# Moving the rotary tables, a diagonal and one accumulator bank in a hybrid attention block

## The chip, the cores and the metric

The kernel runs on one core of a Trainium2 chip. The metric is the device time of one execution in microseconds (us), as the median of several runs; less is better. A core has five engines that run side by side and wait for each other by semaphores: TensorE (PE in the profile, its weight loads PEld) multiplies matrices into eight accumulator banks of 128 x 512 fp32; VectorE (DVE) and ScalarE (ACT) work on tiles of 128 partitions and read the banks; GpSimd (POOL) works on tiles and issues some transfers; SyncE (SP) issues the other transfers.

## What is computed

One block of a model with 512 tokens and 1024 features, all in fp32. Cut to what matters here:

```python
n = rmsnorm(h, g_mix)
gq, gk, gv, gr, z_gf, z_gb, cq, ckv, kr, z_ma, z_mb = split(n @ w_in)
y_gla = gla_branch(gq, gk, gv, gr, z_gf, z_gb, ...)   # 4 heads, gated linear attention, both directions
q = rmsnorm(cq, g_q) @ w_uq                           # 8 heads; 64 plain and 32 rotary features each
kv = rmsnorm(ckv, g_kv) @ w_ukv                       # keys (64) and values (128) of each head
k_rope = rope(kr, positions)                          # one rotary key for all heads
y_mla = softmax(q @ k.T * 96**-0.5) @ v
merged = sigmoid(z_ma) * y_gla + sigmoid(z_mb) * y_mla
h = h + merged @ w_out
h = h + square(relu(rmsnorm(h, g_mlp) @ w_ff1)) @ w_ff2
return rmsnorm(h, g_final)
```

`rope(x)` turns pairs of features by an angle: it needs the cosine and sine of position times frequency.

## The kernel before, in words

Every matrix product is made of three products (`mm3`, lines 87 to 90): each operand is split into a high part, rounded for TensorE's fast format, and the low rest; high x high, high x low and low x high are summed into one bank. A split takes ScalarE for the high part and VectorE (in places GpSimd) for the low one (`split`, lines 92 to 94; `split_scaled`, 96 to 98).

The work goes in this order: the first input projections; the three large ones (gr, za, gv) by a seven-product scheme for 2 x 2 blocks; the four heads of the linear attention (GLA), with the projections of the latents cq and ckv and of the gates in between; the softmax attention (MLA) of eight heads in pairs; the output product with w_out; the two feed-forward products in four quarters.

The change lies where GLA ends and MLA begins, in the straight stretch for the last GLA head, `h = GH - 1` (lines 1305 to 1340). There stand, in the order of the text:

- `ckv_.sums()` (line 803) sums the squares of the key latent into a bank (`ckvss`), and VectorE and GpSimd make 1/rms of it; `ckv_.diagonals()` (line 811) lets VectorE turn these 512 numbers into two diagonal matrices (`ckvdg`, line 292), in five instructions; `ckv_.spread()` (line 818) multiplies them with ones on TensorE, so that the scale of each token stands in every partition (`ckvrs`, line 301); `ckv_.normed()` scales the latent by it and splits it.
- `gla_state(h, keys)` (line 574): 12 matmuls into one bank, and a copy of the bank by ScalarE (`gla3s`, line 584), which `gla_out` reads on TensorE (line 742).
- `rotary.tables()` (line 858): two ScalarE activations, `sin` (860) and `cos` (861), from angles that were made long before. Their function is not in the table that ScalarE holds, so a table load goes ahead; the next tanh (line 380) loads the old table again.
- `over_rms` (line 375) scales the late gates 4 and 5 on VectorE; `rotary_k()` (line 891) turns the rotary key on VectorE, in four instructions that read `sin` and `cos` (lines 894 to 897); `rotary_k_split()` splits it into `kbuf`.
- `rotary_begin`, `rotary_q`, `up_T`, `up_units` (line 1023): loads, splits and products of the rotary query (`ro`), and for each pair of heads of the plain query (`uq`), the key (`uk`) and the value (`uv`); these are units of a generator, so that later pairs can be put between attention steps.
- the gates z_mb of 128 features each: `zb6` and `zb7` are loaded and split by `begin` and run by `proj_run`; `zb7` is the last, run right ahead of the first scores.

What sets the order: up to this stretch's end TensorE, VectorE and ScalarE keep the order of the text (`in_program_order`, lines 1341 to 1343); GpSimd too. In the attention that follows, a scheduler orders the steps, helped by `goes_behind` pairs; from the output product on the order of the text holds again. SyncE's queue is ordered by the scheduler except for a few pairs.

The eight banks are two pools of four by tag, "mm" and "at". Banks are handed out from the free ones when the scheduler comes to the first use; the use waits until the last reader of the bank's earlier tile is done. In the attention the scores (`s`) and the transposed probabilities (`tp`) take "at" banks, the up-projections, the value products (`av`) and GLA's turns (`y`) take "mm" banks. `begin` always takes "mm"; `proj_begin` takes a tag.

Of the kernel before, what the change touches and what calls it, by code (L numbers as in the profile page):

```python
# [18 lines left out]
P = 128  # L19
# [16 lines left out]
C_ZA, C_ZB = 3776, 4800  # L36
# [20 lines left out]
def tile_block(ctx: ExitStack, tc: tile.TileContext, t, out: bass.AP):  # L57
# [10 lines left out]
    def u2(name, dt=F32, shape=(P, S)):  # L68
        return tl(list(shape), dt, "u2", 29, name)
# [7 lines left out]
    def ps(tag, name):  # L77
        serial[0] += 1
        return pp.tile([P, S], F32, tag=tag, bufs=4, name=f"{name}_{serial[0]}")
# [7 lines left out]
    def mm3(acc, lh, ll, rh, rl, start, stop, onto=False):  # L87
        nc.tensor.matmul(acc, lh, rh, start=start, stop=False, skip_group_check=onto)  # L88
        nc.tensor.matmul(acc, lh, rl, start=False, stop=False, skip_group_check=onto)  # L89
        nc.tensor.matmul(acc, ll, rh, start=False, stop=stop, skip_group_check=onto)  # L90
# [16 lines left out]
    def traced():  # L107
        return len(nc.cur_bb.bb.instructions)
# [111 lines left out]
    def weights(src, name):  # L220
        k, w = src.shape
        nk = k // P
        wf = stage(nk, w, name)
        nc.sync.dma_start(wf, src.rearrange("(k p) w -> p k w", p=P))
        wh, wl = halves(nk, w, name)
        split(wh, wl, wf)
        return wh, wl

    w_in = t["w_in"][0]

    def proj_begin(w, col, name, tag="mm"):
        wh, wl = weights(w[:, col : col + P], name)
        return wh, wl, ps(tag, name)

    def begin_late(col, name, tag="mm", w=None):

        wf = stage(KD, P, name)
        nc.sync.dma_start(wf, (w_in if w is None else w)[:, col : col + P].rearrange("(k p) w -> p k w", p=P))
        wh, wl = halves(KD, P, name)
        nc.scalar.activation(wh, wf, AF.Copy)  # L240

        def lows():
            nc.vector.tensor_tensor(wl, wf, raw(wh), op=ALU.subtract)

        return (wh, wl, ps(tag, name)), lows

    def proj_run(begun, src, half=None, ks=range(KD)):
        wh, wl, acc = begun
        c = slice(0, S) if half is None else slice(half * 256, half * 256 + 256)
        for k in ks:  # L250
            mm3(acc[:, c], wh[:, k, :], wl[:, k, :], src[k][:, 0, c], src[k][:, 1, c], k == 0, k == KD - 1)
        return acc
# [120 lines left out]
    def over_rms(acc, name):  # L373
        z = u2(f"z{name}")
        nc.vector.tensor_tensor(z, acc, R, op=ALU.mult)
        return z

    def half_tanh(z, name):
        th = u2(f"t{name}")
        nc.scalar.activation(th, z, AF.Tanh, scale=0.5)  # L380
        return th
# [192 lines left out]
    def gla_state(h, keys):  # L574

        half, at = h // 2, (h % 2) * GDV
        c = slice(at, at + GDV)
        acc = ps("at", f"gla{h}st")
        for j in range(NT):
            tok = slice(j * P, (j + 1) * P)  # L580
            mm3(acc[:, (j // 2) * GDV : (j // 2 + 1) * GDV], keys[:, 0, tok], keys[:, 1, tok],
                v[j, half][:, 0, c], v[j, half][:, 1, c], j % 2 == 0, j % 2 == 1)
        state = u2(f"gla{h}s")
        nc.scalar.activation(state, acc, AF.Copy)
        return state
# [194 lines left out]
    class Latent:  # L780
# [4 lines left out]
        def begin(self, j):  # L785
            self.begun[j] = proj_begin(w_in, self.col + j * P, f"{self.name}{j}")
# [77 lines left out]
    def rotary_begin():  # L864
        res = []
        for x in range(2):
            wf = stage(3, P, f"wr{x}")
            lo = NOPE + x * HALF
            for k in range(3):
                nc.sync.dma_start(  # L870
                    wf[:, k, :].rearrange("p (h e) -> p h e", h=MH), w_uq[:, k, :, lo : lo + HALF]
                )
            wh, wl = halves(3, P, f"wr{x}")
            split(wh, wl, wf)
            res.append((wh, wl))
        return res
# [14 lines left out]
    def rotary_k():  # L891
        r = slice(64, 96)
        sgn = u2("krsin")
        nc.vector.tensor_scalar(sgn[r], sin[r], cst[r, K_SIGN : K_SIGN + 1], None, op0=ALU.mult)
        nc.vector.tensor_tensor(kswap[r], kswap[r], sgn[r], op=ALU.mult)
        nc.vector.tensor_tensor(kr[r], kr[r], cos[r], op=ALU.mult)
        nc.vector.tensor_tensor(kr[r], kr[r], kswap[r], op=ALU.add)
# [285 lines left out]
    ckv_, cq_ = Latent(C_CKV, 2, V_KV, "ckv"), Latent(C_CQ, 3, V_Q, "cq")  # L1183
# [7 lines left out]
    for n, (a, m) in enumerate(steps[:-4]):  # L1191
# [4 lines left out]
        if steps[n + 1] in fillers:  # L1196
            at = traced()
# [57 lines left out]
    rotary = Rotary()  # L1255
    pooled = traced()
    for h in range(GH - 1):
# [6 lines left out]
        if h < 2:  # L1264
            w_b, lows = begin_late(C_GQ + (h + 2) * P, f"gq{h + 2}")
# [30 lines left out]
        else:  # L1296
# [5 lines left out]
            w_b = begin(C_ZB + 5 * P, "zb5")  # L1302
# [4 lines left out]
    ckv_.sums()  # L1307
    zb5 = proj_run(w_b, xT)
    cq = cq_.normed()
    state = gla_state(h, keys)  # L1310
    cos, sin = rotary.tables()
    late = [over_rms(acc, f"b{f}") for f, acc in ((4, zb), (5, zb5))]
    rotary_k()
    ckv_.diagonals()
    wr = rotary_begin()
    zb = begin(C_ZB + 6 * P, "zb6")
    kbuf = rotary_k_split()
# [9 lines left out]
    ro = rotary_q(accs)  # L1327
    zb = over_rms(proj_run(zb, xT), "b6")
    next(units)
    w_b = begin(C_ZB + 7 * P, "zb7")  # L1330
    g2.append(half_tanh(zb, "b6"))
    first_units = traced()
    for n, _ in enumerate(units):
# [3 lines left out]
    at = traced()  # L1337
# [20 lines left out]
    at = traced()  # L1358
# [4 lines left out]
    for n in range(4 * MH + LAG_C - 1):  # L1363
# [12 lines left out]
        if 2 <= n % 8 < 7:  # L1376
            at = traced()
# [5 lines left out]
        if n in (6, 14):  # L1383
            units = up_units(n // 8 + 2)
            at = traced()
# [4 lines left out]
        if n == 30:  # L1390
            xs_ = wo_accs[1] = [ps("mm", f"wox{rb}") for rb in range(2)]
            at = traced()
# [32 lines left out]
        if n == 17:  # L1425
            at = traced()
# [235 lines left out]
    at = traced()  # L1662
# [9 lines left out]
    at = traced()  # L1672
# [7 lines left out]
    at = traced()  # L1680
# [12 lines left out]
    at = traced()  # L1693
# [8 lines left out]
    for qd in range(NQ):  # L1702
# [14 lines left out]
        for n, m in enumerate(ORDER):  # L1717
# [4 lines left out]
            if m == 2:  # L1722
                accs, begin = [ps("mm", f"gw{qd}{rb}") for rb in range(2)], True
# [3 lines left out]
            else:  # L1727
                accs, begin = (zs_, m == 5) if m in (5, 3) else (xs_, m == 1)
# [20 lines left out]
def build(arrays):  # L1749
    nc = bacc.Bacc("TRN2", target_bir_lowering=False, num_devices=1, dynamic_dma_scratch_size=8192)  # L1750
    t = {
        n: nc.dram_tensor(f"in_{n}", list(a.shape), mybir.dt.from_np(a.dtype), kind="ExternalInput").ap()
        for n, a in arrays.items()
    }
    out = nc.dram_tensor("out_0", [1, S, D], F32, kind="ExternalOutput").ap()
    with tile.TileContext(nc) as tc:
        tile_block(tc, t, out)
    return nc
# [16 lines left out]
```

## Time and profile before

| what | value |
|---|---|
| median of 3 runs | 755.55 us (755.13 to 756.49) |
| the profiled execution | 754.4 us, span of its instructions 752.7 us |
| TensorE clock granted | 0.997 of full |
| first scores of the attention begin | 295.62 us into the span |
| HBM read, written | 83.25 MB, 2.10 MB |

How to read the rows further down: the page's first part gives busy time and share of the span by engine. A row of the waits names who waited, for whom, the sum, how often, the longest. A row of the timeline has start and duration in us, engine, line, operation, `out<-in`, the form (partitions x elements), how often in a row, and in brackets how long the engine had been idle before it and what ended that. Matmuls are pipelined: the next one starts before the end that is shown for the last. A row of the stages (windows) has, for each engine, busy us and the number of instructions.

### The profile page before, as it was taken

Reading aid. Unit: us, or ns where it says so; the run is one execution under the profiler, and the core shown is the slowest. Engines: PE = TensorE matmul, PEld = TensorE weight load, DVE = VectorE, ACT = ScalarE, POOL = GpSimd, SP = SyncE. Lnnn points to the kernel's source line nnn. Section 1 sums busy time; section 2 is a strip of 40 time slices with the busy share of each in tenths; the row PEclk is TensorE's granted clock in tenths of the full one; section 3 lists DMA queues with packets and bytes.
Section 4 is the critical chain, followed back from the end, with each engine's and each line's share of the span. In section 5 each row is a group of like instructions: output and inputs, shape, how many; then the busy total and the mean of one; then the engine's idle time right before and its main releaser. Section 6 shows DMA issues by size and latency. Waiting matters only on the chain.

```text
span 752.7 us, 10206 instructions
## 1 busy us (share of the span) xinstructions
PE 742.9 (99%) x3688; PEld 628.0 (83%) x3688; DVE 580.5 (77%) x842; ACT 457.7 (61%) x776; POOL 165.7 (22%) x238
## 2 busy tenths in 40 slices
PE   9999999999999999999999999999999999999996
PEld 7888888888889888899988988888888888888885
DVE  7777886989787577888897688856696578748795
ACT  7557574686567476978865766345644465345644
POOL 0722110262573522246750100000000000000014
PEclk9999999999999999999999999999999999999998
DMA  9859582611322234458798321461126310650003
GB/s 310 263 124 241 168 175 82 113 29 32 80 57 39 39 85 108 110 146 220 222 194 256 115 66 44 154 182 56 57 80 199 115 56 15 198 152 0 29 0 112
DMA packets 94722, 88.90 MB, mean 118 GB/s; under 512 B 15792, under 2 KB 66992, under 8 KB 94672
## 3 DMA queue, kind: packets, MB, share of 16 engines
q1 hardware_dynamic: 88176, 75.64, 33.8%
q0 software_dynamic: 6208, 12.32, 9.3%
q8 instruction: 29, 0.48, 0.3%
q10 hardware_dynamic: 288, 0.28, 0.1%
q14 instruction: 21, 0.17, 0.1%
HBM read 83.25 MB, written 2.10 MB: 113 GB/s over the span
## 4 chain that ended last, share of the span: by engine, by line
PE 95%; DVE 2%; ACT 1%; issue 1%; POOL 0%; POOLq 0%; ACTq 0%
PE f L88 8%; PE f L89 8%; PE f L90 8%; PE gx L88 4%; PE gx L90 4%; PE gx L89 4%; PE first L330 3%; PE tp L1122 2%; PE gz L88 2%; PE gz L90 2%; PE gz L89 2%; PE zb L88 1%; PE zb L89 1%; PE zb L90 1%; PE av L88 1%; PE s L88 1%
## 5 line engine op out<-in xcount | busy, mean ns | idle before, releaser
L1714 POOL DMA_DIRECT2D gfin<-in_g_final x1 | 0.6, 628 | 283.9 <-PE f L90 283.9
L977 DVE TENSOR_TENSOR w<-w,w 128x1024 f32<-128x1024 f32 x32 | 38.7, 1220 | 0.3
L1102 DVE TENSOR_REDUCE top<-s 128x1 f32<-128x512 f32 x32 | 21.9, 684 | 3.6 <-PE s L90 3.0
L1107 ACT ACTIVATE e<-s,top 128x512 f32<-128x512 f32 x32 | 22.0, 688 | 3.5 <-DVE top L1102 3.4
L1452 DVE TENSOR_TENSOR h<-h,gx 128x512 f32<-128x512 f32 x32 | 21.5, 680 | 1.9 <-PE gx L90 1.8
L94 DVE TENSOR_TENSOR pT<-tp,pT 128x512 fp32r<-128x512 f32 x32 | 21.6, 681 | 1.5 <-ACT pT L93 1.5
L93 ACT ACTIVATE pT<-tp 128x512 fp32r<-128x512 f32 x32 | 18.9, 595 | 2.7 <-PE tp L1122 2.5
L1122 PE MATMUL tp<-ident,e 128*128 128x128 f32 x128 | 19.4, 274 | 0.0
L88 PE MATMUL av<-pT,v 128*128 128x256 f32 x64 | 19.1, 298 | 0.0
L93 ACT ACTIVATE ghb<-y 128x512 fp32r<-128x512 f32 x16 | 10.1, 632 | 14.0 <-DVE y L923 14.0
L1518 ACT ACTIVATE fa<-f 128x512 f32<-128x512 f32 x32 | 18.5, 577 | 0.0
L89 PE MATMUL av<-pT,v 128*128 128x256 f32 x64 | 18.2, 285 | 0.0
L90 PE MATMUL av<-pT,v 128*128 128x256 f32 x64 | 18.1, 283 | 0.0
L1122 PEld LDWEIGHTS tp<-ident,e 128*128 128x128 f32 x128 | 15.2, 140 | 3.3 <-ACT e L1113 0.4
L93 ACT ACTIVATE b_00h<-w 128x1024 fp32r<-128x1024 f32 x7 | 7.4, 1060 | 12.6 <-PE gz L90 6.0
L562 ACT ACTIVATE bds<-bd 128x512 f32<-128x512 f32 x4 | 2.4, 597 | 20.5 <-PE bd L545 20.5
L93 ACT ACTIVATE b_10h<-w 128x1024 fp32r<-128x1024 f32 x7 | 7.4, 1060 | 12.1 <-PE gz L90 6.0
L93 ACT ACTIVATE b_20h<-w 128x1024 fp32r<-128x1024 f32 x7 | 7.4, 1059 | 12.1 <-PE gz L90 6.0
L88 PE MATMUL s<-kbuf,q 96*128 96x512 f32 x32 | 14.1, 441 | 0.0
L1527 ACT ACTIVATE px<-fa 128x256 f32<-128x256 f32 x32 | 13.4, 418 | 1.0
L973 POOL DMA_DIRECT2D w<-in_w_out x10 | 12.3, 1406 | 7.6 <-DVE bo60l L94 6.5
L646 POOL DMA_DIRECT2D gvw<-in_w_in x4 | 4.8, 1226 | 38.7 <-DVE gvw L651 34.0
(1769 smaller groups left out, 2917.6 us busy)
## 6 DMA issues: line engine op xcount, KB each, us to landing
w<-in_w_ff SPq DMA_DIRECT2D x64, 256.0 KB, 3.5
w<-in_w_out POOLq DMA_DIRECT2D x10, 512.0 KB, 9.2
grw<-in_w_in SPq DMA_DIRECT2D x8, 512.0 KB, 8.6
zaw<-in_w_in SPq DMA_DIRECT2D x8, 512.0 KB, 7.3
gvw<-in_w_in SPq DMA_DIRECT2D x8, 512.0 KB, 4.5
w<-in_w_out SPq DMA_DIRECT2D x16, 256.0 KB, 5.3
x<-in_xt SPq DMA_DIRECT2D x8, 256.0 KB, 5.1
vw<-in_w_first SPq DMA_DIRECT2D x8, 256.0 KB, 5.3
```

Of the source, the lines that this page charges most:

```text
L88: nc.tensor.matmul(acc, lh, rh, start=start, stop=False, skip_group_check=onto)
L89: nc.tensor.matmul(acc, lh, rl, start=False, stop=False, skip_group_check=onto)
L90: nc.tensor.matmul(acc, ll, rh, start=False, stop=stop, skip_group_check=onto)
L93: nc.scalar.activation(hi, src, AF.Copy)
L94: rest.tensor_tensor(lo, src, raw(hi), op=ALU.subtract)
L330: nc.tensor.matmul(f_accs[i], a[:, i * P : (i + 1) * P], b, start=k == 0 and x == 0, stop=k == KD - 1 and x == 2)
L977: nc.vector.tensor_tensor(wq[dst][g], wq[x][g], wq[y][g], op=op)
L1102: nc.vector.tensor_reduce(top, acc, axis=AX.X, op=ALU.max, negate=True)
L1107: nc.scalar.activation(e, acc, AF.Exp, bias=top, accum_out=tot[:, qt % 2 : qt % 2 + 1])
L1122: nc.tensor.transpose(tp[:, k * P : (k + 1) * P], e[:, k * P : (k + 1) * P], ident)
L1452: nc.vector.tensor_tensor(hc, hc, acc, op=op)
L1518: nc.scalar.activation(a, acc, AF.Relu)
```

## The change

Three edits in the stretch for the last GLA head. `rotary.tables()` now stands ahead of `gla_state`, so ScalarE's table load, sine and cosine stand ahead of its copy of the state. `ckv_.diagonals()` now stands ahead of `rotary_k()` on VectorE. The bank of the last gate, `zb7`, is asked from "at" instead of "mm"; `begin(col, name)` is `proj_begin(w_in, col, name)` with the tag "mm", so nothing else in this call differs.

```diff
@@ -1307,11 +1307,11 @@
     ckv_.sums()
     zb5 = proj_run(w_b, xT)
     cq = cq_.normed()
+    cos, sin = rotary.tables()
     state = gla_state(h, keys)
-    cos, sin = rotary.tables()
     late = [over_rms(acc, f"b{f}") for f, acc in ((4, zb), (5, zb5))]
+    ckv_.diagonals()
     rotary_k()
-    ckv_.diagonals()
     wr = rotary_begin()
     zb = begin(C_ZB + 6 * P, "zb6")
     kbuf = rotary_k_split()
@@ -1327,7 +1327,7 @@
     ro = rotary_q(accs)
     zb = over_rms(proj_run(zb, xT), "b6")
     next(units)
-    w_b = begin(C_ZB + 7 * P, "zb7")
+    w_b = proj_begin(w_in, C_ZB + 7 * P, "zb7", "at")
     g2.append(half_tanh(zb, "b6"))
     first_units = traced()
     for n, _ in enumerate(units):
```

No instruction is added or taken away. With the banks and the order of the stretch, the scheduler's order of the attention changes as well: 133 lines of difference for TensorE, 191 for VectorE, 146 for ScalarE, 12 for SyncE, none for GpSimd.

## The prediction

> **What bounds the kernel now.** I read the page first, its busy line and its chain:
>
> ```profile
> PE 742.9 (99%) x3688; PEld 628.0 (83%) x3688; DVE 580.5 (77%) x842; ACT 457.7 (61%) x776; POOL 165.7 (22%) x238
> PE 95%; DVE 2%; ACT 1%; issue 1%; POOL 0%; POOLq 0%; ACTq 0%
> ```
>
> TensorE is busy for 99% of the span and holds 95% of the chain. An edit that changes no matmul can gain only where PE waits. So the second view is that of PE's own waits; it has three rows in all:
>
> ```profile
> PE warm L320 <- POOL ident masks.py:199: 1.5, 1, 1.5
> PE ckvrs L301 <- DVE ckvdg L292: 1.0, 1, 1.0
> PE zb L88 <- DVE q L98: 0.5, 1, 0.5
> ```
>
> The first is at the start and stays. The other two are what this diff touches: the key latent's row scales (`ckvrs`) wait for VectorE's diagonal, the last late gate (`zb`, weights zb7) waits for a query split. The third view is the busy time by stage, to see what lies around and behind:
>
> ```profile
> 255.00:273.30 18.30, 17.23 (x116) 15.36 (x114) 12.37 (x27) 10.88 (x16) 1.01 (x1) 1.00 0.10 28
> 295.60:320.00 24.40, 24.40 (x150) 21.17 (x149) 19.57 (x36) 21.58 (x49) 5.28 (x8) 1.00 0.46 119
> 320.00:350.00 30.00, 30.00 (x209) 27.48 (x208) 25.71 (x45) 24.32 (x55) 15.79 (x19) 1.00 0.62 166
> 350.00:378.00 28.00, 27.95 (x196) 25.01 (x195) 24.39 (x46) 24.26 (x51) 20.30 (x24) 1.00 0.80 218
> ```
>
> Columns: stage, its length, busy time of PE, PEld, DVE, ACT, POOL, then clock and DMA. PE is idle for 18.30 - 17.23 = 1.07 us ahead of 273.3. In the attention (295.6 to 378) it is idle for 0.05 us, while VectorE has 4.83 + 4.29 + 3.61 = 12.73 us to spare. So nothing is to be gained there, and something can be lost.
>
> **The change part by part.** The timeline around the first wait:
>
> ```profile
> 261.55 1.83 ACT L826 ACTIVATE cqhl<-cqc 128x512 fp32r<-128x512 f32 x3 [1.73 <-DVE cqc L824]
> 264.43 1.28 DVE L375 TENSOR_TENSOR zb<-zb,R 128x512 f32<-128x512 f32 x2
> 266.29 0.60 ACT L584 ACTIVATE gla3s<-gla3st 128x512 f32<-128x512 f32 x1 [2.92 <-PE gla3st L90]
> 266.91 1.28 ACT L860 ACT_TABLE_LOAD   x1
> 268.20 0.63 ACT L860 ACTIVATE sin<-ang 128x512 f32<-128x512 f32 x1
> 268.74 0.71 ACT L861 ACTIVATE cos<-turns,half_pi 128x512 f32<-128x512 f32 x1
> 268.87 0.48 DVE L894 TENSOR_SCALAR krsin<-sin,gvec 32x512 f32<-32x512 f32 x1 [3.15 <-ACT sin L860]
> 269.78 1.89 PE L742 MATMUL gla3o<-gla3s,qk 128*128 128x256 f32 x8
> 271.41 0.16 DVE L812 TENSOR_TENSOR ckvr<-ckvr,r_x 128x4 f32<-128x4 f32 x1
> 271.42 0.62 ACT L93 ACTIVATE kbuf<-kr 32x512 fp32r<-32x512 f32 x1 [0.19 <-DVE kr L897]
> 272.50 0.68 DVE L292 TENSOR_TENSOR ckvdg<-ident,ckvrl 128x512 fp32r<-128x512 f32 x1
> 272.63 1.10 PE L301 MATMUL ckvrs<-ckvdg,ones_r 128*128 128x512 f32 x2 [0.97 <-DVE ckvdg L292]
> 273.10 0.55 DVE L94 TENSOR_TENSOR wr0l<-wr0f,wr0h 128x384 fp32r<-128x384 f32 x1
> 273.58 0.40 PE L88 MATMUL ro<-cqhl,wr0h 128*128 128x512 f32 x1
> 273.82 0.40 PE L89 MATMUL ro<-cqhl,wr0h 128*128 128x512 f32 x1
> ```
>
> The order that it shows: ScalarE stands idle 2.92 us for the state's matmuls, copies the state, then loads the sine table; VectorE stands idle 3.15 us for the sine; the rotary key's four instructions follow, then the five of the diagonal, and PE waits.
>
> *Sine and cosine first.* Moved are one table load and two activations, ahead of the state's 12 matmuls (another engine) and its copy. No DMA goes with them; the built program's POOL order is unchanged. ScalarE is free at 261.55 + 1.83 = 263.38. The three took from 266.91 to 268.74 + 0.71 = 269.45, 2.54 us, so they would end at 265.92. The copy begins at 266.29 as before: 0.37 us of cover. Cost: nothing; gain: ScalarE's next copies, 2.5 us sooner.
>
> What if the table switch is longer than its row? The copy now ends at 266.89 and PE reads the state at 269.78, so a switch longer by T costs PE T - 0.37 - 2.89 us, nothing up to T = 3.26. The Trainium skill, "ScalarE: Activation LUTs", section "What ACT_TABLE_LOAD costs", gives a load of 1.283 us and a drain of 1.38 us with it. The row agrees on the load; no drain stands in this trace, where load and sine follow the copy within 0.02 us each. By that page T would be 1.38 and the sum the same.
>
> *The diagonal ahead of the rotary key.* Nine VectorE instructions change places: the diagonal's five (271.41 to 273.10, 1.69 us) go first, the rotary key's four (268.87 to 271.41, 2.54 us) behind. VectorE is free at 264.43 + 1.28 = 265.71, so the diagonal is done at 267.4, 5.8 us sooner, and the rotary key at 269.95 (sine and cosine are there since 265.92) instead of 271.41: 1.46 us sooner in spite of standing behind. The low weights wr0l follow at 270.5 for 273.65. On ScalarE `kbuf` waits for the rotary key; it and all behind it on both engines come 1.46 us sooner. Without the early sine the diagonal would fit into the 3.15 us wait just as well, but the rotary key would stay where it was; what the first edit buys is that the feeders keep up with a PE that comes sooner.
>
> PE's side: the eight L742 end at 271.67 by the model of 0.38 us each, so their step is (1.89 - 0.38)/7 = 0.215 us and the next matmul could begin at 269.78 + 8 x 0.215 = 271.50. The two of `ckvrs` at 0.24 each (`ro`'s own step, 273.58 to 273.82) let `ro` begin at 271.98 instead of 273.58: **1.60 us**. At least it is the 1.07 us of recorded idle time. `ro` needs wr0h (ScalarE, some 2.5 us sooner) and at its third matmul wr0l at 270.5: nothing is late next.
>
> *The last gate's bank.* Its rows:
>
> ```profile
> 260.57 0.15 DVE L807 SCALAR_TENSOR_TENSOR ckvr<-ckvss,r_x 128x4 f32<-128x4 f32 x1
> 286.57 1.21 DVE L94 TENSOR_TENSOR zb7l<-zb7f,zb7h 128x1024 fp32r<-128x1024 f32 x1
> 289.23 0.69 DVE L98 SCALAR_TENSOR_TENSOR q<-uq,q 64x512 fp32r<-64x512 f32 x1 [0.66 <-ACT q L97]
> 289.31 0.28 PE L90 MATMUL uv<-wk0h,ckvhl 128*128 128x256 f32 x1
> 290.07 0.47 PE L88 MATMUL zb<-xT,zb7h 128*128 128x512 f32 x1 [0.48 <-DVE q L98]
> 290.38 0.39 PE L89 MATMUL zb<-xT,zb7h 128*128 128x512 f32 x1
> 292.01 0.88 DVE L763 SCALAR_TENSOR_TENSOR grb<-gla3o,gla3ss,grb 128x256 f32<-128x256 f32 x2
> ```
>
> Before, the gate's bank is that of `uq`, freed when VectorE's second q split ends at 289.92. In the built program it is now the bank of `ckvss`, last read at 260.57. The last `uv` begins at 289.31; at its 0.12 us step the gate could begin at 289.43 instead of 290.07 (0.64), and its first step is 0.31 instead of 0.24 (0.07): **0.71 us**, at least the 0.48 of the wait row. The weights' low half ends at 287.78, or 286.32 with the 1.46 us; the gate would begin at 289.43 - 1.60 = 287.83: 1.5 us of cover.
>
> The other side of the swap: the first scores move one bank on. s01 now takes a `gla3o` bank, which the gating at 292.01 to 292.89 frees, and that is 1.46 us sooner too, 291.4, while s01 begins near 294 (the gate's 24 matmuls and three of s00 at 0.24 behind 287.83). Not late.
>
> *What moves without being named.* The scheduler orders the attention anew: on VectorE 13 of the 32 score maxima now stand ahead of something that they stood behind, PE takes uq of pair 2 earlier, and SP's two loads of bo20f go behind seventeen other issues. The matmuls stay the same in number. The bo20f loads:
>
> ```profile
> 321.23 0.82 SPq L983 DMA_DIRECT2D bo20f<-in_w_out  x2
> 376.26 1.04 ACT L93 ACTIVATE bo20h<-bo20f 128x1024 fp32r<-128x1024 f32 x1
> ```
>
> Between load and use lie 54 us; seventeen issues like this one (0.82 us for two) take 7. The first place where VectorE is parked:
>
> ```profile
> 302.12 0.68 DVE L98 SCALAR_TENSOR_TENSOR q<-uq,q 128x512 fp32r<-128x512 f32 x1
> 303.04 0.17 DVE L1112 RECIPROCAL tot<-tot 128x2 f32<-128x2 f32 x1 [0.24 <-ACT e L1107]
> 303.60 0.40 PE L90 MATMUL s<-kbuf,q 96*128 96x512 f32 x1
> 303.64 0.68 DVE L94 TENSOR_TENSOR kbuf<-uk,kbuf 128x512 fp32r<-128x512 f32 x1
> 307.33 0.53 SPq L1075 DMA_DIRECT2D kbuf<-kbuf  x1
> 313.15 0.40 PE L88 MATMUL s<-kbuf,q 96*128 96x512 f32 x1
> ```
>
> The maximum of s10 now follows the q split (ends 302.80), but its scores end at 304.00: 1.2 us parked. Then come the maximum (0.68 like the other 512-wide rows) and the 0.60 us of reciprocal and scaling (303.04 to 303.64), so the split of `kbuf` begins at 305.28 instead of 303.64, 1.64 us later. Two chained copies by DMA hang on it, the second issued at 307.33, for scores at 313.15: 5.8 us apart, so 1.64 us is likely covered. I cost the new order at nothing, the nearer to PE's 0.05 us of idle time, and bound it by 0.2 us below (two or three first steps of 0.07 like the gate's that fall away) and 8.6 us above (the second rival).
>
> **Sum.** 1.60 + 0.71 = 2.31 us, at least 1.07 + 0.48 = 1.55. From 295.6 on PE has no idle time worth naming to take it back. The profiled execution took 754.4 us (span 752.7), 1.15 less than the median of the three, 755.55: it would take 752.1, and the median 753.2.
>
> **The rivals.**
> 1. *One new wait inside the attention.* PE's uq of pair 2 comes earlier, while its weight split on ScalarE goes behind two exponentials, four splits and a scaling that it stood ahead of, and POOL's low half follows it:
>
> ```profile
> 305.08 1.00 POOL L94 TENSOR_TENSOR wq2l<-wq2f,wq2h 128x384 fp32r<-128x384 f32 x1 [8.97 <-ACT wq2h L93]
> ```
>
> If PE gets there when the high half has only just come, it waits for the whole split, 1.00 us: 754.2. For it: the distance between this split and its reader shrinks from both ends. Against: 12.73 us of spare VectorE time, and no wait of PE in all 32 blocks before.
> 2. *VectorE becomes the bound of the attention (slower).* Its place is the 13 moved maxima. If each one delays what stood ahead by the 1.64 us worked out for the first, that is 21.3 us; beyond the spare 12.73, PE loses 8.6 us: 755.55 - 2.31 + 8.6 = 761.8. It decides against the gain from an average of (12.73 + 2.31)/13 = 1.16 us. Against: most of the moves go past one instruction, right behind scores that PE has done.
> 3. *It doesn't do what it says.* ScalarE's state copy is held up (T above 3.26), or the gate still waits for another bank or its weights: only one of the two terms is gained, 754.0 (1.60) or 754.8 (0.71).
>
> **How the numbers follow.** Chances: forecast 0.62, first rival 0.20, second 0.12, third 0.06. A difference of 0.2%, 1.5 us, is about what a measurement of this kernel can tell from no change; that is below 754.0 or above 757.1. Faster: 0.59 of the forecast's (the lower bound, 1.55, is just there), 0.05 of the first rival's and 0.02 of the third's, 0.66. Slower: the second rival and little more, 0.13. Same: the rest, 0.21. The range goes from 752.5 (the sum, 0.2 below and 0.5 of scatter, the runs of before being 1.4 us apart) to 755.3 (the first rival with as much again); above it lies the second rival.
>
> **What would show it.** In the changed profile PE's waits should have lost both rows; the sine should follow `cqhl` on ScalarE and end ahead of the state copy at 266.3; `ro` should begin near 272.0, the gate near 287.8, the first scores near 293.3, and the attention should still show PE busy throughout. Wrong would be: a PE wait for a `top`, `e`, `pT` or `wq2l` between 293 and 376, or VectorE with more idle time ahead of its maxima and PE below 99%.

## The result and the profile after

The changed kernel takes **753.29 us** (median of 13 executions, 753.01 to 753.96), the kernel before 755.2 us in the same comparison (13 executions, 754.23 to 756.96): a ratio of 0.9977, 95% interval 0.997 to 0.9985, so 0.15 to 0.30% faster. The profiled execution took 753.01 us, with a span of 751.0 us at a granted clock of 0.999. The forecast was 753.2.

First the two lines of the page that opened the prediction, now of the kernel after:

```profile
PE 741.9 (99%) x3688; PEld 628.3 (84%) x3688; DVE 581.4 (77%) x842; ACT 457.5 (61%) x776; POOL 166.0 (22%) x238
PE 98%; DVE 1%; issue 0%; POOL 0%; ACT 0%; POOLq 0%
```

TensorE's share of the chain rises from 95 to 98%: the other engines hold 3 points less of it. PE's own waits, after:

```profile
PE warm L320 <- POOL ident masks.py:199: 1.5, 1, 1.5
PE av L88 <- DVE tb L1150: 0.9, 1, 0.9
```

Both rows that the change aimed at are gone, and one stands there that before did not have: a value product (`av`) waits for a merge (`tb`). The stages, in the columns of the prediction, their bounds moved along by 1.3 us (2.3 in the attention), show where it is:

```profile
255.00:272.00 17.00, 17.00 (x116) 15.73 (x115) 14.09 (x29) 10.91 (x16) 1.01 (x1) 1.00 0.12 33
293.30:317.70 24.40, 24.40 (x152) 21.43 (x151) 18.76 (x36) 20.45 (x47) 5.08 (x9) 1.00 0.46 122
317.70:347.70 30.00, 30.00 (x210) 27.46 (x209) 26.34 (x48) 25.98 (x59) 16.15 (x20) 1.00 0.64 165
347.70:375.70 28.00, 27.13 (x190) 24.14 (x189) 25.04 (x45) 23.90 (x50) 20.80 (x25) 1.00 0.80 219
```

The first stage has lost its 1.07 us of idle PE. The last stage of the attention had 0.05 us of it and now has 0.87. The timeline of the places that the prediction dated:

```profile
263.50 1.28 ACT L860 ACT_TABLE_LOAD   x1
...
264.79 0.63 ACT L860 ACTIVATE sin<-ang 128x512 f32<-128x512 f32 x1
...
266.40 0.60 ACT L584 ACTIVATE gla3s<-gla3st 128x512 f32<-128x512 f32 x1 [0.37 <-PE gla3st L90]
...
266.81 0.69 DVE L292 TENSOR_TENSOR ckvdg<-ident,ckvrl 128x512 fp32r<-128x512 f32 x1
...
270.07 0.63 ACT L93 ACTIVATE kbuf<-kr 32x512 fp32r<-32x512 f32 x1 [1.30 <-DVE kr L897]
...
271.43 0.81 PE L301 MATMUL ckvrs<-ckvdg,ones_r 128*128 128x512 f32 x2
...
272.07 0.40 PE L88 MATMUL ro<-cqhl,wr0h 128*128 128x512 f32 x1
...
287.90 0.40 PE L88 MATMUL zb<-xT,zb7h 128*128 128x512 f32 x1
...
293.37 0.40 PE L88 MATMUL s<-kbuf,q 96*128 96x512 f32 x1
```

**How two executions are laid over each other.** One execution begins its steady work up to 1.2 us later than another; two of the same kernel lie 0.6 us apart (after and after_again, sine_alone and sine_again). Taken from the state's first matmul of the last GLA head (264.60 in before, 264.71 here), everything up to the change agrees, and differences are the change's own. So read, the first scores come 31.02 us behind that matmul before and 28.66 after: 2.36 us sooner. At the first product of the second output block (`wow`), behind the attention, 1.84 are left, and 1.84 at the end. The 0.5 us between are the subject of most of what follows.

The new wait, on PE and in VectorE's queue:

```profile
371.58 0.68 DVE L1150 SCALAR_TENSOR_TENSOR tb<-tb,av 128x512 f32<-128x512 f32 x1
...
372.25 0.69 DVE L94 TENSOR_TENSOR pT<-tp,pT 128x512 fp32r<-128x512 f32 x1
...
372.34 0.74 POOL L1153 TENSOR_TENSOR mx<-tb,yg 128x256 f32<-128x256 f32 x1 [1.71 <-DVE tb L1150]
...
372.86 0.78 DVE L94 TENSOR_TENSOR gao<-mx,gao 128x512 fp32r<-128x512 f32 x1
...
373.04 1.20 POOL L1153 TENSOR_TENSOR my<-tb,yg 128x256 f32<-128x256 f32 x1
...
373.55 1.23 DVE L94 TENSOR_TENSOR glyo<-yo,ghyo 128x512 fp32r<-128x512 f32 x1
...
374.00 0.39 PE L90 MATMUL wox<-bo10h,gao 128*128 128x512 f32 x1
...
374.71 0.41 DVE L1150 SCALAR_TENSOR_TENSOR tb<-tb,av 128x256 f32<-128x256 f32 x1
...
375.26 0.36 PE L88 MATMUL av<-pT,v 128*128 128x256 f32 x1 [0.87 <-DVE tb L1150]
```

Head 7, the last, is merged in two halves. Both halves of its value product lie in one bank, and the second may not be written before the merge has read the first. That merge (374.71) stands on VectorE behind three low parts of splits, `pT`, `gao` and `glyo`. The third takes 1.23 us here, beside an addition of GpSimd (`my`, 373.04).

### The profile page after: what moved, and what is told of

Same layout as the page of the kernel before. It is cut to its first block, busy times and chain, and to the rows that moved or that the text cites. A ratio compares the mean times of both kernels' runs of the same rounds, so it can differ in the third digit from the quotient of the medians.

```text
span 751.0 us, 10202 instructions
## 1 busy us (share of the span) xinstructions
PE 741.9 (99%) x3688; PEld 628.3 (84%) x3688; DVE 581.4 (77%) x842; ACT 457.5 (61%) x776; POOL 166.0 (22%) x238
## 4 chain that ended last, share of the span: by engine, by line
PE 98%; DVE 1%; issue 0%; POOL 0%; ACT 0%; POOLq 0%
PE f L88 8%; PE f L89 8%; PE f L90 8%; PE gx L88 4%; PE gx L89 4%; PE gx L90 4%; PE first L330 3%; PE gz L88 2%; PE gz L89 2%; PE gz L90 2%; PE tp L1122 2%; PE zb L88 1%; PE zb L89 1%; PE zb L90 1%; PE s L88 1%; PE s L89 1%
## 5 line engine op out<-in xcount | busy, mean ns | idle before, releaser
L88 PE MATMUL av<-pT,v 128*128 128x256 f32 x64 | 19.2, 300 | 0.9 <-DVE tb L1150 0.9
L88 PE MATMUL s<-kbuf,q 96*128 96x512 f32 x32 | 14.1, 439 | 0.0
```

## The experiments

All times are medians; "before" is the kernel before on the same chip. All medians lie within half a per cent of before's, so a median is read together with its interval and with the trace. "Scores" and "end" are the gain in the trace at the first scores and at the last stage, laid over before as above:

| kernel | median, us | before | ratio, 95% | scores | end |
|---|---|---|---|---|---|
| bank_alone | 755.33 | 755.07 | 1.0007 (0.9998 to 1.0015) | 0.74 | 0.21 |
| order_alone | 753.33 | 755.07 | 0.9976 (0.9968 to 0.9985) | 1.64 | 1.64 |
| merge_first | 753.07 | 755.07 | 0.9974 (0.9963 to 0.9985) | 2.35 | 2.12 |
| merge_first_before | 755.75 | 755.07 | 1.0008 (0.9999 to 1.0017) | -1.29 | -1.64 |
| sine_alone | 752.88 | 754.96 | 0.9969 (0.9958 to 0.9981) | 2.35 | 2.38 |
| diag_alone | 754.65 | 754.96 | 0.9997 (0.9988 to 1.0006) | 0.19 | 0.21 |
| relief | 754.94 | 754.96 | 0.9999 (0.999 to 1.0008) | 2.36 | 0.06 |
| cover8 | 757.38 | 754.96 | 1.003 (1.0017 to 1.0042) | -3.41 | -3.90 |
| sine_bank | 753.35 | 755.23 | 0.9976 (0.9965 to 0.9987) | 2.35 | 1.87 |
| sine_again | 752.79 | 755.23 | 0.9966 (0.9954 to 0.9978) | 2.35 | 2.37 |
| after_again | 753.43 | 755.23 | 0.9971 (0.996 to 0.9981) | 2.35 | 1.88 |

**bank_alone**: the kernel before with the last gate's bank alone.

```diff
-    w_b = begin(C_ZB + 7 * P, "zb7")
+    w_b = proj_begin(w_in, C_ZB + 7 * P, "zb7", "at")
```

> Only the last gate's bank is changed; sine, cosine and the diagonal stand as before. The built program already shows the new order of the attention, so the bank brings that order by itself. Theory A (the terms are independent, and the 0.6 us given back behind the first scores belongs to the new order of the attention): the wait for the diagonal stays at 1.0 us, the gate's wait of 0.5 us goes, the first scores come 0.7 us sooner, and the wait of head 7's second value product for VectorE's merge appears here too; about 0.1 to 0.3 us is left of 0.71, 755.0. Theory B (it is given back because TensorE comes sooner to a VectorE that does not): with only 0.7 us gained the wait is 0.2 us or less and 754.5 comes out.

Measured: 755.33 us, no gain. Its PE waits are the old one for the diagonal and the new one for the merge:

```profile
PE ckvrs L301 <- DVE ckvdg L292: 1.0, 1, 1.0
PE av L88 <- DVE tb L1150: 0.9, 1, 0.9
```

PE is only 0.74 us sooner here, and the wait for the merge is as long as with all three edits. So it isn't PE's being sooner that makes it (theory B); it comes with the bank, as A has it.

**order_alone**: sine, cosine and the diagonal first, the gate's bank as before.

```diff
     cq = cq_.normed()
+    cos, sin = rotary.tables()
     state = gla_state(h, keys)
-    cos, sin = rotary.tables()
     late = [over_rms(acc, f"b{f}") for f, acc in ((4, zb), (5, zb5))]
+    ckv_.diagonals()
     rotary_k()
-    ckv_.diagonals()
```

> Sine and cosine first and the diagonal first, the last gate's bank as before; the built program keeps the attention's order of before on TensorE. Theory A: 1.60 us are gained at the diagonal and kept to the end, no wait of head 7's second value product above 0.2 us: 755.2 - 1.6 = 753.6. Theory B: the merge on VectorE is what that product waits for as soon as TensorE is sooner, the order apart; the wait grows to about 0.6 us or more, and 754.2 comes out. In both the gate's wait of 0.5 us stays.

Measured: 753.33 us, 1.64 gained at the scores and 1.64 at the end; one wait but the first row is left, `PE zb L88 <- DVE q L98: 0.5, 1, 0.5`. Theory A again: with the attention's old order nothing is given back. And this kernel is as fast as the one with the third edit.

**merge_first**: the changed kernel, and the split of the third pair's sum y emitted two steps later; VectorE then has the merge ahead of `glyo`.

```diff
-        for x, at in (("y", (18, 26, 34)), ("z", (20, 28, 36))):
+        for x, at in (("y", (18, 26, 36)), ("z", (20, 28, 36))):
```

> The changed kernel with one more edit: the split of the third pair's sum y is emitted two steps later, so that on VectorE the merge of head 7's first half stands ahead of that split's low part and no longer behind it. Theory A (the 0.87 us wait of head 7's second value product is the merge's place in VectorE's queue, behind a subtraction that took 1.23 us): the merge begins at about 373.6 instead of 374.7, ends before TensorE is done with the six matmuls ahead (374.4), the wait row goes and the kernel takes 753.3 - 0.87 = 752.4. Rival: the product waits for something else that ends at the same moment, or the next reader (the third pair's corner on the same queue) is then late; 753.3 stays.

Measured: 753.07 us, between theory A's 752.4 and the rival's 753.3. The wait for the merge is gone, so its cause was the merge's place behind `glyo`. But of the 0.87 us only 0.28 reach the end. Behind the attention PE is 2.93 us ahead of before; at the last output product it waits. The row, the step of VectorE that ends just before, and the busy time of VectorE in the output product ahead of it:

```profile
407.61 1.04 ACT L93 ACTIVATE f00h<-f00f 128x1024 fp32r<-128x1024 f32 x1
...
407.92 0.68 DVE L1452 TENSOR_TENSOR h<-h,wox 128x512 f32<-128x512 f32 x1
...
408.75 0.47 PE L88 MATMUL wox<-bo40h,gdo 128*128 128x512 f32 x1 [0.38 <-ACT f00h L93]
```

```profile
377.00:399.00 22.00, 22.00 (x99) 18.10 (x98) 21.66 (x31) 11.08 (x19) 8.12 (x9) 1.00 1.08 236
```

VectorE is busy for 21.66 of these 22.00 us (before as well: 21.66). The row names ScalarE's split of `f00`, which ends at 408.65, 0.10 ahead; but this product has no use for `f00`. It adds onto the bank that VectorE reads at line 1452, until 408.60: 0.15 ahead, the distance at which the gate followed the q split before (289.92 to 290.07). I take VectorE to be what PE waits for here; its queue through the output product is 1.65 us sooner than before in this kernel, while PE came 2.93 us sooner. Behind that full stretch VectorE does have gaps, in a chain that runs through ScalarE and GpSimd too, but this chain is as long as ever: 7.94 us from the step `woz` at 399.98 to 407.92, and from 400.75 to 408.69 in before.

Part of VectorE's lateness is this edit's own. The same step comes 1.97 us sooner than before in the changed kernel, where the low parts from `glyo` to `bo50l` take 7.49 us in sum, and 1.65 sooner here, where they take 7.82. In sine_alone it comes 2.36 us sooner, as much as PE, and PE doesn't wait.

**merge_first_before**: the same line in the kernel before.

> The kernel before with the same later split of the third pair's sum. Before, that product began 0.15 us behind the end of the merge and 0.2 us behind the step of the matmul ahead. Theory A: so there is at most 0.2 us to gain, 755.0 to 755.2. Rival (the merge's place costs as much in both kernels): 754.4.

Measured: 755.75 us, nothing gained: a little above theory A's 755.0 to 755.2, and the rival's 754.4 is far off. The profiled execution was the slowest of the eleven (757.24 us), so the table's row for it is not the typical one. In it the gate waited 1.7 us for the q split instead of 0.5, and this row tells why:

```profile
282.70 1.13 ACT L93 ACTIVATE wk0h<-wk0f 128x128 fp32r<-128x128 f32 x4 [2.94 <-DMA wk0f<-in_w_ukv]
```

ScalarE stood 2.94 us for a weight load (1.20 in before's profile), with the rotary query's split behind it in the queue. So the second of the two old waits varies with that transfer. Between the scores and `wow` the trace gains 0.24 us, theory A's 0.2; by the end it has lost 0.6 again. VectorE loses ground here as well: it is 1.33 us later than in before at the merge ahead and 2.15 at the step of line 1452 looked at above, where PE was 1.05 later at `wow`.

**sine_alone** and **diag_alone**: one half of order_alone each.

> Only sine and cosine are moved ahead of the state copy; the rotary key stays ahead of the diagonal, the last gate keeps its bank. Theory A (the diagonal was late only because the four instructions ahead of it waited for the sine): with the sine there at 265.4 the rotary key's 2.54 us and the diagonal's 1.69 us end at 270.0, ahead of TensorE's 271.5; the wait row goes and all of the 1.64 us of both edits come from this one alone: 755.1 - 1.6 = 753.5. Rival (as the prediction shared it out, the order on VectorE is what brings the 1.60): some of the wait stays, 754.3 or more.

> Only the diagonal is moved ahead of the rotary key; sine and cosine stay behind the state copy. Theory A: the diagonal fits into VectorE's 3.15 us wait for the sine and is done at 267.5; the rotary key stays at 271.4, the rotary query's low weights follow at 272.0, just ahead of their use at 272.5: all of the 1.64 us come from this edit alone too, 753.5, and the two edits together bring no more than either. Rival (the prediction's reason for the early sine: the feeders do not keep up without it): the query's products wait for their low weights or a later reader waits for the rotary key, 0.5 to 1.5 us, 754.0 to 755.0.

Measured: 752.88 us for the sine alone and 754.65 for the diagonal alone. By the medians the sine alone gives more than both edits, and more than all three (the direct comparison stands further down): no wait of PE but the first is left. That is theory A, and 0.7 us more than it gave at the scores: the gate's wait is gone as well. The rotary key and what hangs on it, down to the last gate, in its second execution (sine_again, its state 0.58 us later than before's):

```profile
268.15 0.68 DVE L897 TENSOR_TENSOR kr<-kr,kswap 32x512 f32<-32x512 f32 x1
...
269.26 0.63 ACT L93 ACTIVATE kbuf<-kr 32x512 fp32r<-32x512 f32 x1
...
269.95 0.68 DVE L292 TENSOR_TENSOR ckvdg<-ident,ckvrl 128x512 fp32r<-128x512 f32 x1
...
286.87 0.69 DVE L98 SCALAR_TENSOR_TENSOR q<-uq,q 64x512 fp32r<-64x512 f32 x1 [0.66 <-ACT q L97]
...
288.37 0.40 PE L88 MATMUL zb<-xT,zb7h 128*128 128x512 f32 x1
```

Left in its old order, VectorE does the rotary key at once and still has the diagonal done at 270.63, ahead of PE's need. ScalarE's copy `kbuf` comes at 269.26 - 0.58 = 268.68, 2.74 us sooner than before (271.42); with the diagonal in front it was 270.07 - 0.11 = 269.96, 1.46 sooner. All behind it on ScalarE follows: the second q split ends at 287.56, and the gate begins at 288.37, with 0.8 us of cover, in its old bank.

The diagonal alone shows the other side. Its waits:

```profile
PE ro L88 <- ACT yg L776: 0.9, 1, 0.9
PE zb L88 <- DVE q L98: 0.7, 1, 0.7
```

The 1.6 us at `ckvrs` are gained, and 1.2 of them lost one product later: the second half of the rotary query needs the bank that ScalarE's `yg` reads, and `yg` stands behind `kbuf` as late as ever (275.43 in a trace that began 1.02 us later, 274.41 before):

```profile
275.43 1.25 ACT L776 ACTIVATE yg<-y,gla_gain 128x512 f32<-128x512 f32 x2
...
276.16 0.50 PE L88 MATMUL ro<-cqhl,wr1h 128*128 128x512 f32 x1 [0.93 <-ACT yg L776]
```

Here theory A falls and the prediction's reason holds, in this kernel: without the early sine the feeders don't keep up.

**relief**: merge_first, with the low parts of two weight splits of the output product on GpSimd.

```diff
-    wo_right[7] = [split_part(B12, 0, "bo7")]
+    wo_right[7] = [split_part(B12, 0, "bo7", nc.gpsimd)]
...
-    wo_right[7].append(split_part(B12, 1, "bo7"))
+    wo_right[7].append(split_part(B12, 1, "bo7", nc.gpsimd))
```

> The changed kernel with the later split of the third pair's sum, and the low parts of two weight splits of the output projection (1.22 us each on VectorE) given to the Pool engine, which is idle there. Theory A (VectorE's queue, busy without a gap from 371 to 399, is what the output projection waits for once TensorE is more than about 2.2 us sooner): the 0.4 us wait ahead of the last output product goes, TensorE keeps the 2.9 us that it had ahead of it, and 755.1 - 2.9 = 752.2 comes out. Rival (the wait is for ScalarE's weight split, which the row names, or what Pool takes it takes from VectorE): 753.1 as without the relief, or more.

Measured: 754.94 us, 1.87 slower than merge_first. It didn't relieve VectorE but held it up:

```profile
394.30 2.64 POOL L94 TENSOR_TENSOR bo70l<-w,bo70h 128x1024 fp32r<-128x1024 f32 x1 [1.64 <-ACT bo70h L93]
...
394.60 5.84 DVE L94 TENSOR_TENSOR gdo<-my,gdo 128x256 fp32r<-128x256 f32 x4
...
396.91 2.57 POOL L94 TENSOR_TENSOR bo71l<-w,bo71h 128x1024 fp32r<-128x1024 f32 x1
...
401.18 0.47 PE L88 MATMUL wox<-bo70h,ghzo 128*128 128x512 f32 x1 [0.62 <-DVE h L1452]
```

Four subtractions that take 1.42 us in merge_first took 5.84 beside GpSimd's two. So the test went the other way from what was meant: VectorE some 2 us later (4.42 lost, 2.4 taken off it), PE with three waits of 0.3 to 0.7 us. It fits VectorE as the limit of this stretch; that a VectorE with less to do would keep the 2.93 us was not shown.

**cover8**: the changed kernel with eight more cosines ahead of the state copy.

```diff
     cos, sin = rotary.tables()
+    for _ in range(8):
+        nc.scalar.activation(cos, rotary.turns, AF.Sin, bias=half_pi, scale=-1.0)
     state = gla_state(h, keys)
```

> The changed kernel with the cosine computed nine times instead of once, ahead of the state copy (the same values, only the work is repeated): eight activations at a step of 0.54 us, 4.3 us more on ScalarE. Theory A (the moved work has 0.37 us of cover ahead of the copy and some 2.9 us between copy and reader): the copy ends at about 271.0 instead of 267.0, TensorE waits some 1.1 us for the state, 753.3 + 1.1 = 754.4. Rival (the tables were not hidden but took something already, so there is no cover): all 4.3 us show, 757.6. Rival (the state copy is not what TensorE waits for): 753.3.

Measured: 757.38 us, 4.1 more than the changed kernel. The time alone lies at the first rival's 757.6 and not at theory A's 754.4; the rows speak for theory A:

```profile
266.34 6.01 ACT L1312 ACTIVATE cos<-turns,half_pi 128x512 f32<-128x512 f32 x8
...
272.25 0.58 ACT L584 ACTIVATE gla3s<-gla3st 128x512 f32<-128x512 f32 x1
...
272.88 3.35 PE L742 MATMUL gla3o<-gla3s,qk 128*128 128x256 f32 x7 [2.58 <-ACT gla3s L584]
```

Each repeat took 0.75 us and not the step of 0.54, so T is 6.01; the prediction's formula gives 6.01 - 0.37 - 2.89 = 2.75 us, and PE waits 2.58. The cover was as counted, within 0.2 us. The rest of the 4.1 us is the clock in part: in the profiled execution (759.0 us) the granted clock fell behind that wait:

```profile
270.00:275.00 5.00, 2.42 (x8) 1.86 (x7) 2.56 (x5) 4.88 (x9) 0.00 (x0) 0.72 0.00 0
275.00:280.00 5.00, 5.00 (x15) 3.90 (x15) 2.94 (x4) 4.97 (x13) 0.00 (x0) 0.59 0.76 182
```

Executions at a mean clock of 0.998 took 757.03, still about 1 us more than the wait explains; that is left open.

**sine_bank, sine_again, after_again**, beside each other on one chip: the sine first with the other bank, the sine first alone, and the changed kernel.

> Sine and cosine first and the last gate in the other bank; the diagonal stays behind the rotary key. Theory A (with the sine early and the rotary key left in front, all that feeds the last gate's old bank is 2.9 us sooner, so the gate no longer waits for it; the other bank has nothing left to bring and only carries the new order of the attention with its wait for head 7's merge): first scores 2.35 us sooner, 0.87 us wait at the second value product, 1.8 us sooner at the end: 755.0 - 1.8 = 753.2, some 0.5 slower than sine and cosine alone. Rival (the two gains add up): 752.3 or less.

> Sine and cosine alone ahead of the state copy, run beside the changed kernel on one chip. Theory A (the move of the diagonal takes back 1.3 us of what the early sine gives the feeders, and the bank takes back 0.5 us): no wait of TensorE but the first, 2.4 us sooner than before in the trace, some 0.5 us faster than the changed kernel. Rival (the lower time was scatter between executions): within 0.2 us of the changed kernel.

> The changed kernel itself, for that comparison: 1.85 us sooner than before in the trace, 0.87 us wait for head 7's merge; 755.0 - 1.85 = 753.15.

Measured: 753.35, 752.79 and 753.43 us. The sine alone lies between 752.34 and 753.33, the changed kernel between 752.93 and 753.96; the medians differ by 0.64 us, the traces by 2.37 - 1.88 = 0.49, less than the scatter but the same way in both; of the 48 pairs of one execution of each, the sine alone is the faster in 42. With the bank added the merge's wait is back (0.9 us) and the sine's advantage gone. **By median and trace the best of the versions is the kernel before with the sine and cosine moved and nothing else**, by some 0.5 us.

## Why the prediction was right, point by point

The time was right: 753.2 forecast, 753.29 measured. The sum behind it was not quite: it is 2.31 us, and 1.84 reached the end. That the number fits to 0.1 us is luck: the base was too high by 0.3 to 0.6 us, because the prediction started from the median of three, 755.55, where the larger comparisons have 754.96 to 755.23, and this made up for the 0.47 that the sum has too much.

- *Sine and cosine at no cost.* Right to the hundredth: 0.37 us of idle time ahead of the copy, the load 0.02 us behind the activation ahead of it, the sine 0.01 behind the load. cover8 measured the cover itself.
- *The diagonal, 1.60 us.* Dated right: done at 267.50, `ro` at 272.07, with the 0.11 of this execution 267.39 and 271.96 for 267.4 and 271.98; order_alone keeps 1.64 to the end. What was wrong is whose gain it is. The prediction entered it under the diagonal's move and gave the sine a helper's part. The runs show the reverse: the sine alone removes this wait and the gate's wait too, the diagonal's move alone gains 0.2, and beside the sine it delays ScalarE's copy `kbuf` of the rotary key by 1.28 us (269.96 for 268.68), which is what kept the gate waiting in order_alone. The prediction had both numbers (a rotary key "1.46 us sooner in spite of standing behind") and didn't work out the case without the move.
- *The bank, 0.71 us.* Right up to the first scores: the gate at 287.90 (287.83 forecast, 0.11 to be taken off), and 2.36 us gained at the scores, 0.72 more than order_alone's 1.64. Not kept.
- *"I cost the new order at nothing."* This is the step that failed. The bank alone reorders the attention (order_alone has the old order), and in that order the merge of head 7's first half comes later on VectorE: from the merge ahead of it to its own start 374.71 - 371.58 = 3.13 us, 2.40 before (376.42 - 374.02). The same three low parts stand between the two merges in both kernels; `pT` and `gao` have changed places, and 0.55 of the 0.73 us is `glyo`, 1.23 for 0.68. The wait of 0.87 us is the first rival's in kind and size, "one new wait inside the attention ~1 us", but at neither of the places named: not weights, not probabilities, but a bank whose second half waits for the reader of the first. On the way there the new order gives 0.32 us (PE is 2.68 us ahead when it reaches the first `wox`), a little more than the 0.2 that the prediction had set as its lower bound. The one delay that it worked out in full came and cost nothing: the split of `kbuf` starts at 303.02 (302.91 with the 0.11 off), 303.64 - 302.91 = 0.73 us sooner than before where the scores are 2.36 sooner. So 1.63 us are lost on VectorE there, for the 1.64 forecast.
- *"From 295.6 on PE has no idle time worth naming to take it back."* True of before, and no protection. The second value product began there 0.15 us behind the end of the merge (376.42 + 0.41, then 376.98, rows below): VectorE was just in time, which no wait row tells.
- *VectorE as bound of the attention (second rival).* It didn't come: 12.73 us of spare time became 24.40 + 30.00 + 28.00 - 18.76 - 26.34 - 25.04 = 12.26. What the rival looked for lies one stage on, in the output product, where VectorE is busy for 21.66 of 22.00 us.
- *It doesn't do what it says.* It did: both rows are gone.

Open, because no experiment changed it alone: why GpSimd's addition and VectorE's `glyo` meet as they do. In before, `glyo` starts ahead of the addition and takes 0.68 us; here it starts 0.51 behind and takes 1.23. Before's rows:

```profile
374.02 0.68 DVE L1150 SCALAR_TENSOR_TENSOR tb<-tb,av 128x512 f32<-128x512 f32 x1
...
374.62 0.69 DVE L94 TENSOR_TENSOR gao<-mx,gao 128x512 fp32r<-128x512 f32 x1
...
374.78 1.12 POOL L1153 TENSOR_TENSOR mx<-tb,yg 128x256 f32<-128x256 f32 x1 [1.21 <-DVE tb L1150]
...
375.22 0.68 DVE L94 TENSOR_TENSOR pT<-tp,pT 128x512 fp32r<-128x512 f32 x1
...
375.82 0.68 DVE L94 TENSOR_TENSOR glyo<-yo,ghyo 128x512 fp32r<-128x512 f32 x1
...
375.87 1.22 POOL L1153 TENSOR_TENSOR my<-tb,yg 128x256 f32<-128x256 f32 x1
...
376.42 0.41 DVE L1150 SCALAR_TENSOR_TENSOR tb<-tb,av 128x256 f32<-128x256 f32 x1
...
376.98 0.36 PE L88 MATMUL av<-pT,v 128*128 128x256 f32 x1
```

bank_alone repeats the second pair (1.23, started 0.51 behind), order_alone the first (0.68, 0.04 ahead). The Trainium skill, "SBUF — State Buffer", section "SBUF: two separate sides", says that VectorE with two inputs in SBUF and GpSimd hold a common port in turn, whoever starts first for the whole instruction. These four traces agree, and the 5.84 us of relief too. So read, the rows suggest how the swap did it: in before GpSimd's first addition `mx` meets `gao`, whose inputs are both in SBUF (where all tiles lie), and takes 1.12 us, so the second one, `my`, comes just behind `glyo`; after the swap `mx` meets `pT`, which has one input in a bank, takes 0.74, and `my` is there ahead of `glyo`. That is argued from four traces; an experiment on this pair alone was not made.

## What to carry to other kernels

When several edits aim at one wait, work out each of them alone and in pairs: here one of three was enough for both waits, and the other two each took back part of it (0.7 us with the diagonal, 0.5 with the bank). An accumulator's tag is an edit to the order of everything behind it where a scheduler hands out the banks, so the steps that come just in time (a 0.15 us lead is not seen in any wait row) have to be looked up in the new order as well. And an engine that is busy without a gap behind the place of a gain has to come sooner with it, or part of the gain is lost there: VectorE did in sine_alone (2.36 us), and less so in merge_first (1.65 for PE's 2.93).

## What the runs showed of the hardware

- GpSimd work beside VectorE's subtractions of two tiles wasn't free here: 1.42 us of VectorE became 5.84 beside two instructions of 2.64 and 2.57 us. Work moved there from a full VectorE made the kernel 1.87 us slower.
- One wait of TensorE of 2.58 us was followed by a granted clock of 0.72 and 0.59 in the next two stretches of 5 us; with waits of up to 0.97 us the stretches shown stayed at 1.00, and so did the stretch of 5 us behind the 1.7 us wait in merge_first_before (295 to 300).
- Eight repeats of one activation into the same tile took 0.75 us each, where two into different tiles followed each other after 0.54.
